# Where a modulation vector is summed: strips of the matmul array, or VectorE beside a feed-forward part; and the order of a product in four strips

## The chip, the cores and the metric

The kernel runs on one core of one Trainium2 chip, in float32 throughout (large products as three float32r products of split operands). The time is device microseconds of that core for one execution of the whole two-layer program; lower is better.

## What is computed

Two layers of a backbone over 512 latent tokens and 256 context tokens, width 1024. Of each layer these lines matter here: the modulation vector `mod` comes from the conditioning alone, and the decays of the gated linear attention (GLA) come from a projection to 32 columns.

```
mod   = (silu(c)     @ w_ada[l] + b_ada[l])          # 1024 -> 6 x 1024, one row
mod_c = (silu(c_ctx) @ w_ada[l] + b_ada[l])          # the context tokens' row
sh_m, sc_m, gt_m, sh_f, sc_f, gt_f = split(mod, 6)
h  = rmsnorm(x, norm_mix[l]) * (1 + sc_m) + sh_m      # hc with mod_c
... = split_projection(h @ w_in[l])                   # g_a: 32 columns, 2 x rank 16
y_a = window_attention(...); y_c = neighbourhood_attention(...)
gf  = log_sigmoid(g_a[:, :16] @ gla_gate_w_fwd + b) / 16   # gb from g_a[:, 16:]
y_b = gla_output(gla_bidirectional(..., gf, gb), g_r)
x = x + gt_m * merge_branches(h, y_a, y_b, y_c, ...)
x = x + gt_f * swiglu(rmsnorm(x, norm_ffn[l]) * (1 + sc_f) + sh_f, w_ffn_in[l], w_ffn_out[l])
```

`w_ada[l]` does not depend on the tokens, so the second layer's `mod` can be computed at any time before that layer's first norm. Units 0 and 1 of six (shift and scale of the first norm) are wanted first; the last, `gt_f`, only in the second layer's feed-forward part.

## The kernel before

Activations lie transposed, 128 channels in partitions and up to 768 tokens along the free axis; a product works through blocks of 128 output columns with `KT` = 8 tiles of the inner dimension. Each weight block is loaded into one of three raw buffers `wr` (line 300), and split into a high part on ScalarE (`wh`, line 323) and a low part on VectorE (`wl`, line 326), two blocks ahead. `gemm` runs three matmuls per inner tile (high x high, high x low, low x high).

The program is a list of items; `run_items` walks it. Small work (norms, GLA, attention) is written as generators that `tick` advances by a clock of the program's own: a matmul adds its columns times 0.417 ns (float32r) or 1 ns (float32), a quarter of it for 32-row strips (line 209). After that a scheduler may still move instructions on each engine's queue, as far as data and buffers allow; each engine then runs its queue in order, SP's loads too. So the order in which the program is built is not the order of the code.

Order of stages: first norm and lead of layer 1; GLA beside the gates' products (`zgates`); attention beside more of these; the merge (`merge_items`), where the three branches are weighted and projected out; the feed-forward part (`ffn_items`); then the second layer. The second layer's lead, `gla_lead`, overlaps the end of the first layer's feed-forward part: the norm of the latent tokens, the inner-rank product `gemm_low` on 512 tokens, key and query products, then the same on 256 tokens.

**The modulation vector.** `ada(l, units)` makes for each unit of 1024 columns eight raw items, one for each inner tile: a load of 128 x 1024 (512 KB) through `wr`, and four matmuls of 256 columns with the silu'd conditioning (`cpad`, 32 columns of which two are filled) as the stationary operand, each in its own 32-column strip of the array. They add up in one PSUM buffer `g` over the eight items. Then ScalarE copies the sum (`ada`), and `ada_cols` turns it into columns with two matmuls by `k_sel`. `weave` spreads the items among weighted ones. For the second layer, units 0 and 1 lie in the first layer's attention and units 2 to 5 in the second layer's GLA; the first layer's own units lie in its start and its GLA.

**The inner-rank product.** `gemm_low` takes the weight block `w_ga` (raw, 32 columns for each inner tile) and for each inner tile multiplies the high and then the low half of the activations, in strip `kt % 4`; the four strips' sums are added later by the decays' product with `gw`, whose rows repeat. High and low of one tile thus stand next to each other in one strip.

In the merge, `split` (lines 1487 to 1490 and 168, 169) prepares the first branch's four tiles: a sigmoid on ScalarE, two multiplies on VectorE, a rounded copy on ScalarE, and the remainder on VectorE; the first products wait for them. In a norm, `rstd_rows` (lines 597 to 601) is a chain of small VectorE steps on the token sums, and `norm` (lines 643 to 655) scales and splits tile by tile.

## Time and profile before

| | us |
|---|---|
| median of 3 runs (2550.47 to 2551.61) | 2550.47 |
| the profiled execution, in all | 2551.31 |
| its span | 2549.5 |
| TensorE busy in it | 2477.0 |
| VectorE busy | 1370.3 |
| ScalarE busy | 1040.4 |

The span runs from the first to the last instruction of the program; 1.8 us lie around it. In the profile PE is TensorE, PEld its weight loads (which run beside the matmuls), DVE VectorE, ACT ScalarE, POOL GpSimd and SP the queue that issues the loads. A float32 matmul leaves two records, so four matmuls are x8 in a timeline. Matmuls overlap in their records: what one costs is read from the distance of the starts, not from its length. In tile names `g` and `h` are PSUM buffers of products, `o` and `s` of small work, `T` activations.

### The profile page before, as it was taken

The numbers are of one execution on the slowest core, as the hardware profiler recorded it, in microseconds if no ns is written. First come the engines' busy times: TensorE is split into PE (matmuls) and PEld (weight loads), VectorE is DVE, ScalarE is ACT, GpSimd is POOL, SyncE is SP. The second block draws the span as 40 slices with busy tenths as digits, with TensorE's granted clock in tenths as the row PEclk, the third lists the DMA queues.
The fourth block names the chain that finished last, engine by engine and source line by source line (L and its number), as shares of the span: only waits on it lengthen the run. The fifth ranks groups of instructions, "written<-read, shape, count | busy, mean of one in ns | idle before, by whom it ended". The sixth has DMA issues, their size and how long they took to land.

```text
span 2549.5 us, 39666 instructions
## 1 busy us (share of the span) xinstructions
PE 2477.0 (97%) x15548; PEld 2082.1 (82%) x15548; DVE 1370.3 (54%) x2814; ACT 1040.4 (41%) x1717; POOL 344.4 (14%) x439
## 2 busy tenths in 40 slices
PE   6999999999999999999999999999999999999998
PEld 3777888888888888888888867677888879988887
DVE  4765457647656673222322367646657668633336
ACT  3643345546564452212212245435545566422223
POOL 0231113203213010000000022212313210000000
PEclk9999999999999999999999999899999999999999
DMA  6433543232346332121121344444333276433223
GB/s 229 137 121 116 179 142 98 93 106 81 89 158 221 124 117 90 58 67 66 59 67 62 98 132 133 153 162 119 102 93 86 82 231 191 156 93 99 92 94 120
DMA packets 116427, 300.53 MB, mean 118 GB/s; under 512 B 21520, under 2 KB 31504, under 8 KB 116240
## 3 DMA queue, kind: packets, MB, share of 16 engines
q1 hardware_dynamic: 116240, 297.99, 36.3%
q8 instruction: 122, 2.00, 0.3%
q14 instruction: 65, 0.53, 0.1%
HBM read 258.61 MB, written 29.57 MB: 113 GB/s over the span
## 4 chain that ended last, share of the span: by engine, by line
PE 83%; DVE 8%; ACT 3%; DMA 3%; issue 1%; SPq 1%; POOL 0%; DVEq 0%; ACTq 0%; POOLq 0%
PE g L211 45%; PE h L211 26%; PE s L211 6%; PE s L215 3%; PE o L211 3%; DVE wl L326 1%; DMA wr<-in_w_merge_dram 1%; ACT wh L323 1%; DMA wr<-in_w_in_dram 1%; DVE qd L915 1%; DVE SS L925 0%; DMA T<-zd 0%; DVE T L645 0%; DVE T L582 0%; DVE P L1288 0%
## 5 line engine op out<-in xcount | busy, mean ns | idle before, releaser
L211 PE MATMUL g<-T,wh 128*128 128x512 f32 (+1 forms) x4684 | 1239.3, 352 | 9.1 <-ACT T L720 4.5
L211 PEld LDWEIGHTS g<-T,wh 128*128 128x128 f32 x4684 | 802.1, 190 | 131.1 <-issue 15.8
L211 PE MATMUL g<-T,wl 128*128 128x512 f32 (+1 forms) x2342 | 814.3, 348 | 2.7 <-DVE wl L326 2.5
L211 PE MATMUL h<-T,wh 128*128 128x512 f32 (+1 forms) x2612 | 659.2, 343 | 5.0 <-ACT T L168 4.8
L323 ACT CAST wh<-wr 128x1024 fp32r<-128x1024 f32 (+2 forms) x355 | 344.4, 971 | 711.5 <-PE h L211 263.9
L326 DVE TENSOR_TENSOR wl<-wr,wh 128x1024 fp32r<-128x1024 f32 (+2 forms) x355 | 406.8, 1146 | 380.5 <-ACT wh L323 364.2
L211 PEld LDWEIGHTS h<-T,wh 128*128 128x128 f32 x2612 | 449.6, 189 | 71.4 <-ACT T L168 6.8
L211 PEld LDWEIGHTS g<-T,wl 128*128 128x128 f32 x2342 | 444.8, 190 | 61.6 <-DVE wl L326 4.4
L211 PE MATMUL h<-T,wl 128*128 128x512 f32 (+1 forms) x1306 | 446.3, 342 | 2.5 <-DVE wl L326 2.5
L211 PEld LDWEIGHTS h<-T,wl 128*128 128x128 f32 x1306 | 246.4, 189 | 33.2 <-DVE wl L326 2.9
L1267 ACT ACTIVATE P<-P,sm 128x513 f32<-128x513 f32 (+3 forms) x160 | 115.9, 725 | 127.7 <-DVE sm L1309 113.3
L1272 POOL TENSOR_SCALAR P<-P,sm 128x512 f32<-128x512 f32 (+1 forms) x160 | 112.3, 703 | 387.4 <-DVE sm L1271 357.7
L1322 DVE TENSOR_TENSOR ptl<-s,pth 128x512 fp32r<-128x512 f32 (+1 forms) x144 | 107.9, 749 | 39.0 <-ACT pth L1321 37.8
L652 POOL TENSOR_TENSOR T<-T,T 128x256 f32<-128x256 f32 (+1 forms) x24 | 30.0, 1272 | 731.2 <-DVE T L1552 532.0
L1321 ACT CAST pth<-s 128x512 fp32r<-128x512 f32 (+1 forms) x144 | 90.6, 629 | 46.9 <-PE s L215 43.5
L1552 DVE SCALAR_TENSOR_TENSOR T<-h,mod,T 128x512 f32<-128x512 f32 (+1 forms) x64 | 38.4, 599 | 109.9 <-PE h L211 109.3
L215 PE MATMUL s<-k_ident,P 128*128 128x128 f32 x640 | 94.0, 273 | 1.7 <-POOL P L1272 1.2
L173 ACT CAST T<-T 128x512 fp32r<-128x512 f32 (+1 forms) x93 | 49.1, 536 | 106.7 <-DVE T L1571 100.0
L918 POOL TENSOR_TENSOR E<-E,T 128x512 f32<-128x512 f32 (+1 forms) x42 | 58.4, 1401 | 239.6 <-ACT E L914 212.0
L215 PEld LDWEIGHTS s<-k_ident,P 128*128 128x128 f32 x640 | 74.7, 140 | 16.3 <-issue 4.7
L211 PE MATMUL o<-pth,V 128*128 128x512 f32 (+2 forms) x224 | 72.4, 332 | 0.2 <-ACT pth L1321 0.2
L211 PE MATMUL o<-ptl,V 128*128 128x512 f32 (+2 forms) x224 | 70.8, 332 | 1.1 <-DVE ptl L1322 1.1
(200 smaller groups left out, 2253.7 us busy)
## 6 DMA issues: line engine op xcount, KB each, us to landing
wr<-in_w_fi_dram SPq DMA_DIRECT2D x98, 512.0 KB, 3.5
wr<-in_w_ada_dram SPq DMA_DIRECT2D x80, 512.0 KB, 4.2
wr<-in_w_in_dram SPq DMA_DIRECT2D x65, 512.0 KB, 3.8
wr<-in_w_merge_dram SPq DMA_DIRECT2D x48, 512.0 KB, 4.2
wr<-in_w_out_dram SPq DMA_DIRECT2D x32, 512.0 KB, 3.6
wr<-in_w_fo_dram SPq DMA_DIRECT2D x32, 512.0 KB, 3.5
wr<-in_w_br_dram SPq DMA_DIRECT2D x48, 256.0 KB, 3.0
wr<-in_w_fo_dram SPq DMA_DIRECT2D x32, 384.0 KB, 3.0
```

Source lines behind the costliest of these rows:

```text
L173: self.nc.scalar.copy(hi, src)
L211: return self.nc.tensor.matmul(out, lhsT, rhs, **kw)
L215: return self.nc.tensor.transpose(out, src, self.ident)
L323: self.nc.scalar.copy(hi[:, :n], r[:, :n])
L326: self.nc.vector.tensor_tensor(out=lo[:, :n], in0=r[:, :n], in1=hi[:, :n].bitcast(F32), op=ALU.subtract)
L652: nc.gpsimd.tensor_tensor(out=t[:, w], in0=x[kt][:, w], in1=r[:, w], op=ALU.mult)
L918: P.tensor_tensor(out=ee[:, 1, c0:c1], in0=ee[:, 1, c0:c1], in1=self.gk[p][:, t0:t0 + c1 - c0], op=ALU.mult)
L1267: nc.scalar.activation(out=P_[:, o0:e1], in_=P_[:, o0:e1], func=AF.Exp, bias=nm_, accum_out=rz)
L1272: nc.gpsimd.tensor_scalar(out=P_[:, o0:o1], in0=P_[:, o0:o1], scalar1=rz, scalar2=1.0, op0=ALU.mult, op1=ALU.mult)
L1321: nc.scalar.copy(hi, src)
L1322: return lambda: VE.tensor_tensor(out=lo, in0=src, in1=hi.bitcast(F32), op=ALU.subtract)
L1552: self.nc.vector.scalar_tensor_tensor(out=x[:, c0:c1], in0=ps[:, :c1 - c0], scalar=self.mod[l][:, sec * 8 + j, s:s + 1], in1=x[:, c0:c1], ...
```

## The change

`ada` is no longer called for the second layer. In its place a generator `ada_late` is started in the first layer's feed-forward part, after the first two weight pairs. For each unit, half of its columns (512) and inner tile it loads 128 x 512 (256 KB) into one of two buffers `wad`, and VectorE multiplies it by the tile's conditioning value, a scalar per partition, once for the latent and once for the context row: a multiply for the first inner tile, a multiply-add into `wac` for the other seven. After eight tiles the 128 partitions are added on TensorE: for each of the two rows four matmuls of 128 columns in the four strips, by `sel`, which has one column of ones. ScalarE copies the result, and after both halves `ada_cols` turns it into columns as before. Between the steps the generator asks for 4.5 of the program's clock.

In `gemm_low` the eight inner tiles go in two halves of four; in each, the four high halves go to the four strips in turn, then the four low halves. The number of matmuls is the same.

```diff
--- before.py
+++ after.py
@@ -423,6 +423,11 @@
         self.cpad = self.cp.tile([128, KT, 32], F32, name="cpad")
         nc.gpsimd.memset(self.cpad, 0.0)
         nc.scalar.activation(out=self.cpad[:, :, 0:2], in_=cs, func=AF.Silu)
+
+        self.sel = self.cp.tile([128, 2, 32], F32, name="sel")
+        nc.gpsimd.memset(self.sel, 0.0)
+        for s in range(2):
+            nc.gpsimd.memset(self.sel[:, s, s:s + 1], 1.0)
         self.mod = [self.cp.tile([128, 48, 2], F32, name=f"mod{l}") for l in range(DEPTH)]
         self.gain = [self.cp.tile([128, 2, 8, 2], F32, name=f"gain{l}") for l in range(DEPTH)]
         self.nmix, self.nffn, self.bada, self.bmerge, self.gbias, self.gnorm, self.sink = ([] for _ in range(7))
@@ -485,6 +490,47 @@
                     self.tick()
                 self.items.append(Item(fn, self.a["w_ada"][l, n, kt], 8, raw=True))
 
+    def ada_late(self, l):
+
+
+        nc = self.nc
+        sb = None
+        todo = [(n, h, kt) for n in range(6) for h in range(2) for kt in range(KT)]
+
+        def load(q):
+            n, h, kt = todo[q]
+            t = self.ph.tile([128, 512], F32, tag="wad", name=self.nm("wad"), bufs=2)
+            nc.sync.dma_start(t, self.a["w_ada"][l, n, kt][:, 512 * h:512 * h + 512])
+            return t
+        w = load(0)
+        for q, (n, h, kt) in enumerate(todo):
+            nxt = load(q + 1) if q + 1 < len(todo) else None
+            if kt == 0:
+                acc = self.ph.tile([128, 2, 512], F32, tag="wac", name=self.nm("wac"), bufs=1)
+            for s in range(2):
+                c = self.cpad[:, kt, s:s + 1]
+                if kt == 0:
+                    nc.vector.tensor_scalar(out=acc[:, s], in0=w, scalar1=c, scalar2=None, op0=ALU.mult)
+                else:
+                    nc.vector.scalar_tensor_tensor(out=acc[:, s], in0=w, scalar=c, in1=acc[:, s], op0=ALU.mult,
+                                                   op1=ALU.add)
+            w = nxt
+            yield 4.5
+            if kt < KT - 1:
+                continue
+            ps = self.gemm_psum()
+            for s in range(2):
+                for g in range(4):
+                    self.matmul(ps[32 * g:32 * g + 32, :128], self.sel[:, s], acc[:, s, 128 * g:128 * g + 128],
+                                start=s == 0, stop=s == 1, tile_position=(0, 32 * g))
+            if h == 0:
+                sb = self.base.tile([128, 256], F32, tag="ada", name=self.nm("ada"), bufs=1)
+            nc.scalar.copy(sb[:, 128 * h:128 * h + 128], ps[:, :128])
+            yield 1.5
+            if h == 1:
+                self.ada_cols(l, n, sb, True)
+                yield 0.5
+
     def adp_tile(self):
         if not self.begun:
             return self.pp.tile([128, 512], F32, tag="a", name=self.nm("a"), bufs=1)
@@ -496,13 +542,14 @@
             return self.pp.tile([128, 512], F32, tag="h", name=self.nm("h"))
         return self.ps.tile([128, 512], F32, tag="g", name=self.nm("g"), bufs=3)
 
-    def ada_cols(self, l, n, sb):
+    def ada_cols(self, l, n, sb, late=False):
+
         nc = self.nc
         pm = self.O1()
 
         for j in range(2):
-            self.matmul(pm[:, :16].rearrange("p (g j s) -> p j g s", j=2, s=2)[:, j], sb[:, j * 128:j * 128 + 128],
-                        self.c["k_sel"], start=True, stop=True)
+            o = pm[:, 8 * j:8 * j + 8] if late else pm[:, :16].rearrange("p (g j s) -> p j g s", j=2, s=2)[:, j]
+            self.matmul(o, sb[:, j * 128:j * 128 + 128], self.c["k_sel"], start=True, stop=True)
 
         def gain(sec, b0, b1):
             j = (SC_M, SC_F).index(sec)
@@ -751,12 +798,14 @@
             mov = self.hmov(l, 0, c)
             n = c[1] - c[0]
             ps = self.gemm_psum()
-            for kt in range(KT):
-                xh, xl = mov(kt)
-                r, s = slice(32 * (kt % 4), 32 * (kt % 4) + 32), slice(32 * kt, 32 * kt + 32)
-                for x, first, last in ((xh, kt < 4, False), (xl, False, kt >= 4)):
-                    self.matmul(ps[r, :n], w[:, s], x.bitcast(F32), start=first, stop=last,
-                                tile_position=(0, 32 * (kt % 4)))
+
+            for half in range(2):
+                hl = [mov(kt) for kt in range(4 * half, 4 * half + 4)]
+                for x in range(2):
+                    for g in range(4):
+                        r, s = slice(32 * g, 32 * g + 32), slice(128 * half + 32 * g, 128 * half + 32 * g + 32)
+                        self.matmul(ps[r, :n], w[:, s], hl[g][x].bitcast(F32), start=half == 0 and x == 0,
+                                    stop=half == 1 and x == 1, tile_position=(0, 32 * g))
             self.ahead()
             if c[0] == 0:
                 tile_()
@@ -1586,6 +1635,8 @@
             for c in sets:
                 for t in range(lead):
                     pair(t, [c])
+            if lead and l < DEPTH - 1:
+                self.do(lambda: self.add(self.ada_late(l + 1)))
             for t in range(t0 + lead, t0 + tn):
                 pair(t, subs_of)
             w = lambda j: self.a["w_fo"][l, j][:, t0 * 128:(t0 + tn) * 128]
@@ -1690,7 +1741,7 @@
             self.do(begin)
             if l == 0:
                 self.do(self.consts_rest)
-            side = self.cap(lambda: self.ada(l, range(2, 6)))
+            side = self.cap(lambda: self.ada(l, range(2, 6))) if not last else []
             main = self.cap(lambda: (self.gla_items(l), self.zgates(l, range(0, ZS[l][0]), ntok)))
             self.weave(main, side)
 
@@ -1702,11 +1753,10 @@
                 self.ztag = "z"
                 self.attn_open(l)
             self.do(to_attn)
-            side = self.cap(lambda: self.ada(1, (0, 1))) if not last else []
             main = self.cap(lambda: (self.attn_a_items(l), self.gate_r(l), self.zgates(l, range(*ZS[l]), ntok),
                                      self.attn_c_items(l, ntok),
                                      self.zgates(l, range(ZS[l][1], 24), ntok)))
-            self.weave(main, side)
+            self.items += main
             self.do(self.close_phase)
             self.do(self.ada_flush)
             self.merge_items(l, (lambda: a["xT"]) if l == 0 else (lambda: self.xs[0]), ntok)
```

How the built program's order changes is shown at three places. On VectorE at the start of the first layer's merge, where the four tiles of the first branch are split (multiplies by `gnorm` and by the result, and the remainder with shape 128x768), the order before is:

```order
L169 TENSOR_TENSOR T_7817<-T_7796,T_7816 128x768
L1488 SCALAR_TENSOR_TENSOR T_7804<-T_7804,gnorm_728,T_7820 128x768
L1490 TENSOR_TENSOR T_7797<-T_7797,T_7804 128x768
L169 TENSOR_TENSOR T_7825<-T_7797,T_7824 128x768
L1488 SCALAR_TENSOR_TENSOR T_7807<-T_7807,gnorm_728,T_7828 128x768
L1490 TENSOR_TENSOR T_7798<-T_7798,T_7807 128x768
L169 TENSOR_TENSOR T_7833<-T_7798,T_7832 128x768
L1488 SCALAR_TENSOR_TENSOR T_7810<-T_7810,gnorm_728,T_7836 128x768
L1490 TENSOR_TENSOR T_7799<-T_7799,T_7810 128x768
L169 TENSOR_TENSOR T_7841<-T_7799,T_7840 128x768
```
and now:

```order
L169 TENSOR_TENSOR T_7707<-T_7686,T_7706 128x768
L1537 SCALAR_TENSOR_TENSOR T_7694<-T_7694,gnorm_732,T_7710 128x768
L1539 TENSOR_TENSOR T_7687<-T_7687,T_7694 128x768
L169 TENSOR_TENSOR T_7715<-T_7687,T_7714 128x768
L513 TENSOR_SCALAR wac_9736<-wad_9732,cpad 128x512 x2
L1537 SCALAR_TENSOR_TENSOR T_7697<-T_7697,gnorm_732,T_7718 128x768
L515 SCALAR_TENSOR_TENSOR wac_9736<-wad_9734,cpad,wac_9736 128x512
L1539 TENSOR_TENSOR T_7688<-T_7688,T_7697 128x768
L515 SCALAR_TENSOR_TENSOR wac_9736<-wad_9734,cpad,wac_9736 128x512
L515 SCALAR_TENSOR_TENSOR wac_9736<-wad_9776,cpad,wac_9736 128x512
L169 TENSOR_TENSOR T_7723<-T_7688,T_7722 128x768
L1537 SCALAR_TENSOR_TENSOR T_7700<-T_7700,gnorm_732,T_7726 128x768
```
Eight of the new steps stand between the second and the fourth tile's remainder (five in these rows, three behind them); each pair needs its load.

On VectorE in the second layer's lead, from the last squares of the context tokens (`T`, 128x256) through the small chain of the root (`nsm`), the order before is:

```order
L582 TENSOR_TENSOR T_13253<-T_13253,T_13745 128x256
L326 TENSOR_TENSOR wl_13759<-wr_13699,wh_13758 128x1024
L1552 SCALAR_TENSOR_TENSOR T_8515<-g_13748,mod_75,T_8515 128x256
L582 TENSOR_TENSOR T_13253<-T_13253,T_13774 128x256
L597 TENSOR_SCALAR nsm_13819<-o_13816 128x2
L185 TENSOR_SCALAR nsm_13819<-nsm_13819 128x2
L188 TENSOR_TENSOR nsm_13819<-nsm_13819 128x2
L189 SCALAR_TENSOR_TENSOR nsm_13819<-nsm_13819 128x2
L190 SCALAR_TENSOR_TENSOR nsm_13819<-nsm_13819 128x2
```
and now (line numbers of the changed file):

```order
L629 TENSOR_TENSOR T_13610<-T_13610,T_14141 128x256
L513 TENSOR_SCALAR wac_14162<-wad_13990,cpad 128x512 x2
L326 TENSOR_TENSOR wl_14155<-wr_14084,wh_14154 128x1024
L1601 SCALAR_TENSOR_TENSOR T_8405<-h_14144,mod_79,T_8405 128x256
L515 SCALAR_TENSOR_TENSOR wac_14162<-wad_14160,cpad,wac_14162 128x512
L629 TENSOR_TENSOR T_13610<-T_13610,T_14175 128x256
L515 SCALAR_TENSOR_TENSOR wac_14162<-wad_14160,cpad,wac_14162 128x512
L644 TENSOR_SCALAR nsm_14224<-o_14221 128x2
L515 SCALAR_TENSOR_TENSOR wac_14162<-wad_14217,cpad,wac_14162 128x512
L185 TENSOR_SCALAR nsm_14224<-nsm_14224 128x2
L326 TENSOR_TENSOR wl_14243<-wr_14172,wh_14242 128x1024
L188 TENSOR_TENSOR nsm_14224<-nsm_14224 128x2
```
The steps on `wac` of the last half unit stand ahead of that chain and inside it, and two weights' low parts have come with them.

On TensorE in the second layer's lead, at the first inner-rank product (strips of 32 rows, 512 columns), high and low half of a tile alternate before:

```order
L211 MATMUL h_13785<-T_13609,wr_13603 32x512
L211 MATMUL h_13785<-T_13610,wr_13603 32x512
L211 MATMUL h_13785<-T_13621,wr_13603 32x512
L211 MATMUL h_13785<-T_13622,wr_13603 32x512
L211 MATMUL h_13785<-T_13637,wr_13603 32x512
L211 MATMUL h_13785<-T_13638,wr_13603 32x512
L211 MATMUL h_13785<-T_13656,wr_13603 32x512
L211 MATMUL h_13785<-T_13657,wr_13603 32x512
```
and now four tiles' high halves stand ahead of their low halves:

```order
L211 MATMUL g_14186<-T_13994,wr_13984 32x512
L211 MATMUL g_14186<-T_14006,wr_13984 32x512
L211 MATMUL g_14186<-T_14022,wr_13984 32x512
L211 MATMUL g_14186<-T_14041,wr_13984 32x512
L211 MATMUL g_14186<-T_13995,wr_13984 32x512
L211 MATMUL g_14186<-T_14007,wr_13984 32x512
L211 MATMUL g_14186<-T_14023,wr_13984 32x512
L211 MATMUL g_14186<-T_14042,wr_13984 32x512
```
So two neighbours no longer share a strip.

## Rows read from the trace of the kernel before

**Rows 1.** The page, part 1: engine, busy us, share of the span, instructions.
```profile
PE 2477.0 (97%) x15548; PEld 2082.1 (82%) x15548; DVE 1370.3 (54%) x2814; ACT 1040.4 (41%) x1717; POOL 344.4 (14%) x439
```

**Rows 2.** Busy time by stretches: stretch, its length, engines, clock, DMA share, GB/s.
```profile
775.00:1445.00 670.00, 666.92 (x3823) 584.53 (x3822) 266.69 (x389) 189.06 (x278) 30.69 (x24) 1.00 0.28 91
...
1516.00:1707.00 191.00, 180.90 (x1496) 132.76 (x1495) 110.41 (x207) 78.78 (x107) 36.37 (x28) 0.92 0.46 153
```

**Rows 3.** TensorE's timeline: start, length, engine, line, tiles, shapes; `ada` items of layer 2.
```profile
412.91 0.64 PE L211 MATMUL g<-wr,cpad 128*32 128x256 f32 x8
413.48 0.73 PE L211 MATMUL g<-T,wh 128*128 128x512 f32 x2
...
1552.52 0.40 PE L211 MATMUL g<-T,wh 128*128 128x256 f32 x2
1552.76 0.28 PE L211 MATMUL g<-T,wl 128*128 128x256 f32 x1
1552.97 1.07 PE L211 MATMUL g<-wr,cpad 128*32 128x256 f32 x16
1553.97 0.50 PE L211 MATMUL g<-T,wh 128*128 128x512 f32 x1
```

**Rows 4.** TensorE's timeline at the start of the first layer's merge.
```profile
750.40 0.64 PE L211 MATMUL g<-wr,cpad 128*32 128x256 f32 x8
751.59 0.58 PE L211 MATMUL o<-k_sel,ada 128*128 128x8 f32 x4 [0.55 <-ACT ada L483]
753.35 0.50 PE L211 MATMUL h<-T,wh 128*128 128x512 f32 x1 [1.18 <-ACT T L168]
```

**Rows 5.** TensorE's timeline: four float32 matmuls of 128 columns, and the next.
```profile
1473.86 1.13 PE L211 MATMUL o<-dg,ones 128*128 128x128 f32 x8 [0.23 <-DVE dg L601]
1474.75 0.36 PE L211 MATMUL h<-T,wl 128*128 128x256 f32 x1
```

**Rows 6.** VectorE's timeline: a multiply and a multiply-add of 128x512.
```profile
73.42 0.42 DVE L885 TENSOR_SCALAR qd<-T 128x512 f32<-128x512 f32 x1
...
1482.55 0.74 DVE L645 SCALAR_TENSOR_TENSOR T<-T,gain,T 128x512 f32<-128x512 f32 x1
```

**Rows 7.** The first merge's start: VectorE, SP's queue; DMA issues by size, us to landing.
```profile
757.11 0.96 DVE L169 TENSOR_TENSOR T<-T,T 128x768 fp32r<-128x768 f32 x1 [0.90 <-ACT T L168]
...
761.95 0.96 DVE L169 TENSOR_TENSOR T<-T,T 128x768 fp32r<-128x768 f32 x1 [1.95 <-ACT T L168]
...
755.52 2.42 SPq L1457 DMA_DIRECT2D T<-zd  x5
...
wr<-in_w_br_dram SPq DMA_DIRECT2D x48, 256.0 KB, 3.0
...
T<-zd SPq DMA_DIRECT2D x24, 384.0 KB, 4.8
```

**Rows 8.** The second layer's lead: VectorE ahead of the second norm.
```profile
1496.08 0.42 DVE L582 TENSOR_TENSOR T<-T,T 128x256 f32<-128x256 f32 x1 [1.57 <-ACT T L581]
1498.43 0.16 DVE L597 TENSOR_SCALAR nsm<-o 128x2 f32<-128x2 f32 x1 [1.93 <-PE o L211]
```

**Rows 9.** Waits of TensorE from 1516 to 1707 us: total, times, longest.
```profile
PE g L211 <- ACT wh L323: 4.3, 4, 2.3
...
PE s L211 <- DVE T L896: 1.8, 1, 1.8
PE g L211 <- DVE wl L326: 1.5, 2, 1.2
```

**Rows 10.** The inner-rank product in the second layer: TensorE, then VectorE.
```profile
1484.71 4.65 PE L211 MATMUL h<-T,wr 128*32 128x512 f32 x22
1490.30 0.62 PE L211 MATMUL h<-T,wr 128*32 128x512 f32 x2 [0.94 <-DVE T L655]
...
1491.96 0.68 DVE L655 TENSOR_TENSOR T<-T,T 128x512 fp32r<-128x512 f32 x1
```

**Rows 11.** A stretch at the lower clock in the second layer's GLA (columns as in rows 2).
```profile
1647.00:1667.00 20.00, 20.00 (x89) 15.28 (x89) 5.60 (x11) 3.22 (x4) 1.33 (x1) 0.50 0.10 31
```

## The prediction

> **What bounds the kernel now.** I read the busy times of the engines first: TensorE is busy 2477.0 of 2549.5 us and VectorE 1370.3 [rows 1]. So a microsecond of TensorE work is worth a microsecond wherever TensorE does not wait, and VectorE has room on average. The average hides stages, so next the table by stretches [rows 2]: from 775 to 1445 us (the end of the first layer's merge and its feed-forward part) TensorE is busy 666.92 of 670 us and VectorE 266.69; from 1516 to 1707 (the second layer's gated linear attention, GLA) TensorE is busy 180.90 of 191 at a mean granted clock of 0.92. Third come the single matmuls of the modulation vector, fourth the places where TensorE waits. The diff takes TensorE work out of the first layer's attention and the second layer's GLA, and puts VectorE work and a little TensorE work into the feed-forward part, which has 403 us of idle VectorE.
>
> **What is removed.** One item of `ada` is four strip matmuls of 256 columns, eight records in the trace. A pair of items starts 0.21 us after the matmul ahead of it, where two such matmuls take 0.24 (1552.52 to 1552.76), and the next weights' matmul starts 1.00 later: 1.09 for two, 0.55 each [rows 3]. One item alone holds TensorE 0.57, and with the same 0.09 ahead 0.66. The second layer's six units are 48 items. 16 (units 0 and 1) lie one by one in the first layer's attention; the last, at 750.40, stands ahead of TensorE's waits of 0.55 and 1.18 us [rows 4] and is hidden, so 15 x 0.66 = 9.9. The other 32 lie in the second layer's GLA, by the program's order 26 in pairs and 6 alone: 26 x 0.55 + 6 x 0.66 = 18.3. Four of the six column turns (`k_sel`, 0.58 us each at 751.59 [rows 4], 0.6 with its start) go out of these stages too, one from attention and three from GLA: 2.4. Together 30.6 us, in stages where TensorE waits little.
>
> **What is added on TensorE.** Twelve sums over partitions, each eight strip matmuls of 128 columns with `sel`, and the six column turns, all in or next to the feed-forward part, where TensorE never stands. The trace has no such sum. A float32 matmul of 128 columns over the whole array takes 0.22 (eight records, 1473.86 to 1474.75 [rows 5]), so eight take 0.44 if four strips run side by side and 1.78 one after another, plus the start. As columns they are what one item was, so I take the lone item's 0.66, the row nearest to them: 12 x 0.66 = 7.9 (bounds 6 to 23). With 6 x 0.6 = 3.6 for the turns 11.5 us. Net of this and the removal: **-19.1 us**.
>
> **What is added on VectorE.** 96 half tiles, each multiplied by two scalars: for one unit's half 2 multiplies and 14 multiply-adds, the first 0.42 and the second 0.74 us by the rows of the same shapes [rows 6]: 11.2 us, 134 in all. In the feed-forward part that is hidden: VectorE has 403 us to spare, the weights' low parts are made two weights ahead, and one weight there is 48 matmuls at 670 / 3823 us each [rows 2], 8.4 us, far more than two steps of 0.74. If the cover were gone, every step would cost its 0.74. ScalarE's twelve small copies in place of six lie in the same stretch (189 of 670 us busy), and three memsets on GpSimd (14% busy [rows 1]) come at the program's start. But the order is not that of the code: the scheduler has moved the first unit's half up to the merge's start and the last one down into the second layer's lead.
>
> The **merge's start** (first layer) is a place where TensorE waits for VectorE and ScalarE: it waits 1.18 for the first tile's split [rows 4], and VectorE idles 1.95 ahead of the third [rows 7]. In the changed order VectorE has eight of the new steps between the second and the fourth tile's low part, and the loads of the second to fifth tile stand on SP's queue, with two buffers, each behind VectorE's release. The gates' loads go out at 755.52 and take 4.8 us at the median for 384 KB; 256 KB take 3.0 [rows 7]. So the first tile lands at about 759.5 where VectorE is ready at 758 (after the second tile's low part, 757.11), then two multiplies (0.8), two to four multiply-adds (0.7 net of overlap) minus the idle time that is there: the fourth split is about 3.5 us late, and so are the gate loads queued behind. Bounds: 1.3 (the two steps ahead of the third tile alone) and 8 (two of the loads waited for in full). **+3.5**.
>
> In the **second layer's lead** sixteen steps stand on VectorE from the end of the first norm on, some inside the small chain that makes the second norm's root, for which VectorE idles 1.57 and 1.93 in the run before [rows 8]. Eight of them (2 x 0.42 + 6 x 0.7 = 5.0) come before the second norm's scaling, three more inside it (2.1); less those 3.5 of idle time and with about 1 us for the sum at the end: **+4.5** (1 to 8). This half unit is wanted only in the second layer's feed-forward part; its cost is its place alone.
>
> **What goes with the removal.** In GLA TensorE waits 4.3 for a weight's high part and 1.5 for its low part [rows 9]: the items share the three raw buffers with the weights. Without them most of that goes: **-4** (0 to -5.8). What is late next is GLA's own chain: its steps are spaced by the program's clock, in which an item counted 0.26 us though it took 0.55 to 0.66, so each step loses some 0.3 to 0.4 us of cover. One such wait of 1.8 is there already [rows 9]: **+3** (0 to 15, if the chain ended every step).
>
> **The inner-rank product.** Before, 11 strip matmuls of 512 columns take 4.65 us (22 records), 0.42 each: two side by side at most, since high and low half of a block follow each other in one strip [rows 10]. Then TensorE waits 0.94 for the norm, whose last low half comes at 1492.64. With four strips in turn TensorE only arrives earlier at that wait; what it does meanwhile is the next weight's matmuls, which are there in both orders. I count 0.5 us for each of the second layer's two calls and 0.5 for the first layer's second: **-1.5** (0 to -10). [...]
>
> **Sum.** -19.1 + 3.5 + 4.5 - 4 + 3 - 1.5 = -13.6. The profiled execution took 2551.3 us in all (span 2549.5); 2551.3 - 13.6 = 2537.7, **2538 us**. The median is 2550.5, 0.8 below the profiled execution, too little to shift it. Less than 0.2% (5 us) either way I call no change.
>
> **Rivals.**
> [...]
> (b) *A wait in place of the one removed* (0.18): GLA's chain keeps half to all of the 18.3, 9 to 18, so 6 to 15 come back beyond the 3 counted: 2544 to 2553. For it: 110 of 191 us on VectorE and the 1.8 wait; against: 1.8 is the only one of its kind there.
> (c) *The clock, slower* (0.11): in this GLA the granted clock stands at 0.50 from 1647 to 1667 us [rows 11], and the mean of 0.92 over 191 us makes it 30 us in all, after strip and 64-wide products and a wait of 1.8 us. If the steps without cover wait like that at each scan and product, half the time in such a stretch is lost: with 40 us more at 0.50 the cost is 20, and 2538 + 20 = 2558. It decides from 36 us more on. [...]
> (d) *The strips do not overlap* (0.06): the new sums run one after another, 12 x (1.96 - 0.66) = 15.6 more: 2554, no change.
>
> **How the numbers follow.** Forecast 0.50, all of it faster; (a) 0.15 faster; (b) 0.07 faster, 0.11 same; (c) 0.11 slower; (d) 0.05 same, 0.01 slower. Faster 0.72, same 0.16, slower 0.12. The range runs from somewhat under (a), 2524, well into (b), 2551: left out are (c), (d) and the outer part of (b), 0.2 together.
>
> **What would show it.** In the changed trace: no `cpad` matmul in the first layer's attention or the second layer's GLA; twelve groups of `sel` strips of about 0.66 us each (serial ones: near 2); a busy VectorE from 775 to 1445 near 390 us with TensorE still full; a longer wait than 1.18 to 1.4 at the merge's start; a wait for VectorE at the second norm of the lead; in GLA fewer waits on high and low weight parts and a stage some 19 us shorter, at a granted clock not below 0.92. I am wrong if the feed-forward part grows by much more than 11 us (VectorE or SP held weights up), if GLA shrinks by under 10, or if its clock falls.

## The result, and the profile after

The changed kernel takes **2517.56 us** (median of 4 runs, 2517.06 to 2520.49), the kernel before beside it 2550.54 (2550.47 to 2551.61): ratio 0.987, 95% interval 0.9853 to 0.9888. It is 33 us faster, where I had forecast 13.6 and a range that ended at 2524. The profiled execution of the changed kernel took 2517.52 us, its span is 2515.7; that is 33.8 less than the profiled execution of before, and the ledger below is made of these two.

Part 1 of the page of the changed kernel answers [rows 1]; the line of part 5 is the new multiply-add (count, busy time, mean ns, idle time ahead and what ended it):

```profile
PE 2441.8 (97%) x15356; PEld 2068.8 (82%) x15356; DVE 1484.7 (59%) x3006; ACT 1043.1 (41%) x1723; POOL 345.9 (14%) x442
...
L515 DVE SCALAR_TENSOR_TENSOR wac<-wad,cpad,wac 128x512 f32<-128x512 f32 x168 | 119.1, 747 | 24.1 <-DMA wad<-in_w_ada_dram 23.8
```

TensorE is 35.2 us less busy, VectorE 114.4 us more. Next the stretches that answer [rows 2] in the changed kernel: the feed-forward part, the second layer's GLA, and three short stretches inside that GLA (stretch, length, busy time of PE, PEld, DVE, ACT, POOL, clock, DMA share, GB/s):

```profile
927.00:1472.00 545.00, 544.77 (x3249) 475.64 (x3248) 273.81 (x410) 128.20 (x196) 3.45 (x4) 1.00 0.35 111
...
1529.00:1717.00 188.00, 178.02 (x1380) 142.36 (x1378) 122.57 (x226) 84.83 (x114) 39.20 (x33) 0.97 0.28 87
...
1546.77:1550.18 3.41, 3.41 (x9) 2.64 (x8) 1.65 (x6) 3.25 (x5) 0.06 (x1) 0.50 0.06 23
1560.42:1563.83 3.41, 3.41 (x12) 2.83 (x11) 3.41 (x9) 0.00 (x0) 0.00 (x0) 0.50 0.00 0
1574.07:1577.48 3.41, 3.41 (x13) 2.89 (x12) 1.07 (x2) 2.28 (x3) 1.88 (x3) 0.50 0.07 22
```

The feed-forward part stays full (544.77 of 545). GLA has become 188 us long, and its granted clock is 0.97 instead of the 0.92 of [rows 2]: all that stands at half rate there now (0.50: a 512-column product starts every 0.43 us, as from 1547.24 to 1547.67, and at full rate every 0.23) are these three stretches, 10.2 us; before, it was 30.7.

Where the 33.8 us come from, stage by stage. The marks are the first matmul of a kind in each stage (the first with `gw`, the first with a `Q`, the first of the merge, the norms' `dg`, 910.2 and 1473.9 before); "at half" is the time at 0.50 in the stage. Two products change stage by the built order, and the table is set right for that: 21 of the gates' 512-column matmuls, 0.23 us each, stand ahead of GLA's mark now and behind it before (4.8 us, left out of both columns), and 24 of 256 columns have crossed the mark between the first layer's GLA and its attention, which are therefore one line. Most of one pair of items (1.0 us, at 1524.6) stands just ahead of GLA's mark before, so its removal is in the lead's line.

| stage | before (at half) | after (at half) | difference |
|---|---|---|---|
| start, up to the first layer's GLA | 82.6 (6.8) | 79.8 (6.8) | -2.7 |
| first layer's GLA, attention, up to the merge's first product | 670.8 (10.2) | 658.3 (3.8) | -12.5 |
| merge, up to the feed-forward part's first norm | 156.9 (0) | 159.7 (6.5) | +2.8 |
| feed-forward part | 563.6 (0) | 573.9 (0) | +10.3 |
| second layer's lead | 51.7 (0) | 52.2 (0) | +0.4 |
| second layer's GLA | 220.2 (30.7) | 188.4 (10.2) | **-31.8** |
| from there to the end | 799.0 | 798.6 | -0.4 |

### The profile page after: what moved, and what is told of

Same layout as the page of the kernel before. It is cut to its first block, busy times and chain, and to the rows that moved or that the text cites. A ratio compares the mean times of both kernels' runs of the same rounds, so it can differ in the third digit from the quotient of the medians.

```text
span 2515.7 us, 39662 instructions
## 1 busy us (share of the span) xinstructions
PE 2441.8 (97%) x15356; PEld 2068.8 (82%) x15356; DVE 1484.7 (59%) x3006; ACT 1043.1 (41%) x1723; POOL 345.9 (14%) x442
## 5 line engine op out<-in xcount | busy, mean ns | idle before, releaser
L211 PEld LDWEIGHTS g<-T,wh 128*128 128x128 f32 x4672 | 801.9, 190 | 118.4 <-issue 13.6
L515 DVE SCALAR_TENSOR_TENSOR wac<-wad,cpad,wac 128x512 f32<-128x512 f32 x168 | 119.1, 747 | 24.1 <-DMA wad<-in_w_ada_dram 23.8
L1601 DVE SCALAR_TENSOR_TENSOR T<-h,mod,T 128x256 f32<-128x256 f32 (+1 forms) x67 | 40.0, 597 | 85.6 <-PE h L211 85.5
```

The costliest lines, as they stand in the source:

```text
L211: return self.nc.tensor.matmul(out, lhsT, rhs, **kw)
L515: nc.vector.scalar_tensor_tensor(out=acc[:, s], in0=w, scalar=c, in1=acc[:, s], op0=ALU.mult, op1=ALU.add)
L1601: self.nc.vector.scalar_tensor_tensor(out=x[:, c0:c1], in0=ps[:, :c1 - c0], scalar=self.mod[l][:, sec * 8 + j, s:s + 1], in1=x[:, c0:c1], ...
```

## The experiments

My theory before them: the forecast's terms hold, and the missing 20 us lie in the second layer's GLA, where the granted clock no longer falls for so long. Rivals: the new order of the inner-rank product did it; attention gained more than its items cost; the strip matmuls themselves bring the clock down; the loads through the weights' buffers do.

### One part at a time

Units 0 and 1 alone summed late:

```diff
...
-                self.do(lambda: self.add(self.ada_late(l + 1)))
+                self.do(lambda: self.add(self.ada_late(l + 1, (0, 1))))
...
-            side = self.cap(lambda: self.ada(l, range(2, 6))) if not last else []
+            side = self.cap(lambda: self.ada(l, range(2, 6)))
```


> Units 0 and 1 alone are summed late (the strips' new order is in); units 2 to 5 stay as items in the second layer's GLA. Theory (the unforecast part sits in the second layer's GLA, because its items are gone, as granted clock and weight waits): attention -13, the start of layer 1 -4.6, merge +5, four sums and two turns in the feed-forward part +3.5, the GLA of layer 2 as in the kernel before with its 30 us at half rate: about 2541 us (2537 to 2545). Rival (the new order of the inner-rank product changes what follows, and so the GLA's clock, whatever the items do): GLA shorter by 10 here already, 2531. Rival (attention gained more than the 9.9 + 0.6 that the items cost): attention 13 or more shorter here, as in the full change; if it depends on GLA it is not.

Units 2 to 5 alone:

```diff
...
+                self.do(lambda: self.add(self.ada_late(l + 1, range(2, 6))))
...
-            self.items += main
+            self.weave(main, self.cap(lambda: self.ada(1, (0, 1))) if not last else [])
```


> Units 2 to 5 alone are summed late; units 0 and 1 stay as items in the first layer's attention. Theory: the second layer's GLA is 36 us shorter, as in the full change (its stretches at half rate 10 us instead of 30), feed-forward part +7, merge start and lead as in the full change +5 and +5, attention unchanged, start -4.6: about 2527 us (2523 to 2531). Rival (the shorter GLA comes from something ahead of it, in attention or the lead, not from its own items): GLA only 18 to 20 us shorter, 2543.

Only the inner-rank product's new order in the kernel before, and all but that order in the changed kernel (the same edit, one way and the other):

```diff
-            for kt in range(KT):
-                for x, first, last in ((xh, kt < 4, False), (xl, False, kt >= 4)):
...
+            for half in range(2):
...
+                for x in range(2):
+                    for g in range(4):
...
```


> The kernel before with only the new order of the inner-rank product. Theory: -1.5 to -6, all of it in the first layer's start and GLA and in the two calls of the second layer's lead: 2544 to 2549 us; the second layer's GLA unchanged with 30 us at half rate. Rival (the order brings the GLA its clock): 2535 or less. [...]

> The changed kernel with the old order of the inner-rank product (high and low half of a tile in the same strip). Theory: it is worth 1.5 in the second layer's lead and the 2.7 to 4.6 by which the first layer's start and GLA are earlier: 2520 to 2524 us, GLA of the second layer as short as in the changed kernel, at a granted clock of 0.97. Rival (the new order brings the GLA its clock): half rate back to some 30 us there, 2532 or more. Rival (the strips overlapped before already): 2517.5 to 2518.5.

Raw marks are those of each kernel, with the 21 products where they stand; on them GLA is 225.0 long in the kernel before and 188.4 in the changed one.

| | median us | ratio to before, 95% | GLA, raw marks (at half) |
|---|---|---|---|
| units 0, 1 late | 2540.19 | 0.9937 to 0.9967 | 214.8 (10.2) |
| units 2 to 5 late | 2520.30 | 0.9854 to 0.9913 | 189.1 (6.8) |
| new product alone | 2545.54 | 0.9959 to 0.9991 | 214.8 (13.7) |
| all but the new product | 2522.58 | 0.9864 to 0.9920 | 189.4 (10.2) |

The medians of the first, third and fourth lie where the theory put them. The second came out 3 us below its range: the lead, which I had down for +5, gave 1.0 there, since 64 steps end ahead of it. GLA falls to 189 whenever its own items are gone, with the old product too, and to no such value otherwise: the product's order and attention are out as causes. In the first layer the stages up to the merge are 11.2 us shorter with units 0 and 1 gone and 2.0 without that, of which 1.7 are half rate.

In two of these profiles the items are in GLA and the half rate is short (10.2 and 13.7). They are the second fastest of 10 runs (2533.6) and the fastest of 10 (2537.8), 7 us below their medians, so they show that the long half rate can stay away, not that it usually does. That needed repeats.

### Is the half rate chance?

> The kernel before unchanged, for a second profile of its second GLA. Theory (the half rate there is there in most executions, since its waits are the same in each): 25 us or more at half rate in GLA and 2549 to 2556 us. Rival (the 30.7 us of the first profile were chance): 10 to 15 us at half rate in GLA at a time of 2540 to 2545.

> As e_before_2, a third profile of the kernel before. The two together with the first tell how far time and half rate go together: by the theory that the time differs between executions through the granted clock alone, the time less half of all half rate is the same within 1.5 us in all three (2551.3 less half of 58.3: 2522.2).

> The changed kernel unchanged, a second profile. Theory: half rate in its second GLA near 10 us again (3 to 14), time 2517 to 2521; if it reaches 25 us or more, the difference of the clock between the two kernels was chance.

The kernel before took 2556.08 and 2552.20 us in these, the changed one 2517.53. GLA stood at half rate for 30.7 us in both profiles of before, in the same three pieces (6.8, 3.4, 20.5) as in the first, and for 10.2 in that of the changed kernel, again three of 3.4. So the difference belongs to the kernels. The other executions on record say how firmly: of 48 of the kernel before, 44 ran at a granted clock of 0.985 to 0.990 over the whole program (2545.3 to 2559.5 us) and four at 0.991 to 0.994 (2540.6 to 2545.0); all five of the changed kernel stood at 0.991 to 0.994. Units 0 and 1 late and the new product alone, which keep the items in GLA, stood at 0.990 or less in 8 of 10 each. The long half rate is thus usual in the kernel before, not certain; no profile is of one of its four fastest executions.

Time less half of all half rate is 2522.2, 2523.0 and 2520.9 in the three of before (2.1 apart, somewhat more than I allowed) and 2498.0 in both of the changed kernel: 24 us of the 34 are there at full clock. Over the 48 executions, whose times lie 19 us apart, the time less the clock's share (one less the granted clock, times the span) lies between 2518.0 and 2525.4. (The ledger at the end gives the clock more than the other 10, since the changed kernel's new 6.8 us at half rate at the merge's start cost nothing there, as a run below shows.)

The stretches of the second profile of before, GLA and its three pieces (columns as above):

```profile
1529.00:1755.00 226.00, 213.52 (x1661) 159.82 (x1659) 128.16 (x233) 88.72 (x120) 39.33 (x33) 0.93 0.46 149
1544.60:1551.40 6.80, 5.40 (x13) 4.35 (x14) 4.93 (x9) 4.81 (x6) 1.79 (x1) 0.50 0.26 80
1626.50:1629.90 3.40, 3.40 (x9) 2.63 (x9) 2.79 (x7) 0.00 (x0) 0.90 (x1) 0.50 0.75 202
1650.40:1670.80 20.40, 20.40 (x90) 15.20 (x89) 4.72 (x8) 3.22 (x4) 1.32 (x1) 0.50 0.14 49
```

And TensorE's timeline at the long piece in that profile (start, length, engine, line, tiles, shapes, wait ahead of it and what ended it):

```profile
1647.38 0.40 PE L211 MATMUL g<-T,wl 128*128 128x512 f32 x1
1649.59 0.46 PE L211 MATMUL s<-T,PP 64*128 64x128 f32 x2 [1.81 <-DVE T L896]
1649.97 0.87 PE L211 MATMUL g<-T,wh 128*128 128x512 f32 x2
...
1651.63 0.79 PE L211 MATMUL s<-gst,SS 64*128 64x128 f32 x2
...
1653.07 0.79 PE L211 MATMUL s<-gst,PP 64*128 64x128 f32 x2
1653.66 0.63 PE L211 MATMUL s<-gst,SS 64*128 64x128 f32 x2
1654.22 0.79 PE L211 MATMUL s<-gv,A 128*128 128x128 f32 x2
...
1666.19 1.13 PE L211 MATMUL s<-qd,E 64*64 64x64 f32 x32
1667.25 0.79 PE L211 MATMUL g<-T,wh 128*128 128x512 f32 x1
...
1671.33 0.40 PE L211 MATMUL g<-T,wl 128*128 128x512 f32 x1
```

TensorE waits 1.81 us for VectorE right ahead of GLA's state products (`PP`, `SS`, `gst`, 64 and 128 rows by 128 columns). At 1650.4, while four of the gates' products run behind the first `PP`, the clock falls to 0.50. The row of small products from 1651.63 to 1667.25 runs at half rate, and the clock rises at 1670.9, when the gates' 512-column products have been running again since 1667.25. This wait is the one of 1.8 in [rows 9], this stretch that of [rows 11].

In the changed kernel the same state products have no wait ahead of them. Its wait of that kind (1.37) stands 47 us earlier, among the gates' products:

```profile
1590.29 0.62 PE L211 MATMUL g<-T,wh 128*128 128x512 f32 x2
1592.29 0.84 PE L211 MATMUL s<-gv,E 128*64 128x128 f32 x10 [1.37 <-DVE T L945]
...
1638.98 0.48 PE L211 MATMUL s<-T,PP 64*128 64x128 f32 x2
1639.30 0.38 PE L211 MATMUL s<-gst,SS 64*128 64x128 f32 x2
1639.62 0.49 PE L211 MATMUL s<-gv,A 128*128 128x128 f32 x2
1640.04 0.48 PE L211 MATMUL s<-gst,PP 64*128 64x128 f32 x2
```

From a `PP` product to the `SS` product behind it it takes 0.32 here and 0.59 above: the same products at the two clocks. The changed kernel still waits in this GLA (total, times, longest), longer at a time than in [rows 9], and for its own chain alone:

```profile
PE s L215 <- POOL SS L1004: 3.0, 2, 2.3
PE s L215 <- DVE gv L854: 2.6, 1, 2.6
PE s L215 <- ACT T L767: 2.3, 1, 2.3
PE s L211 <- DVE T L945: 1.4, 1, 1.4
```

A fall to 0.50 follows each of the first three, but each time the gates' products come next, and it lasts 3.4 us.

Such a wait is not always followed by a fall. In the kernel with the shorter step (below) TensorE waits 2.56 us ahead of the same `SS` product, and the granted clock is 1.00 from 1560 to 1600:

```profile
1571.02 0.44 PE L215 MATMUL s<-k_ident,SS 128*128 128x128 f32 x2 [2.56 <-POOL SS L1004]
...
1560.00:1600.00 40.00, 34.74 (x317) 27.71 (x316) 32.85 (x63) 14.43 (x22) 16.77 (x11) 1.00 0.20 60
```

Nor did one follow waits of 2.27 us (all but the new product), 2.35 (own buffers, below) and 2.09 (step and tie, below). The length of a wait alone does not decide.

### Matmuls or loads?

The items' two halves, put back into the changed kernel's GLA one at a time: the strips without loads, the loads without strips, and whole items with buffers of their own.

```diff
...
+    self.matmul(self.adp[r, :256], self.cpad[:, kt, :], self.cpad.rearrange("p k s -> p (k s)"), ...
...
```


> The changed kernel, and in the second layer's GLA 32 items as before put back as matmuls alone: four strips of 256 columns each on a tile that is already there, no loads, and every eighth followed by the copy to ada; their sums are not used. Cost of the matmuls themselves 32 x 0.55 to 0.66 = 18 to 21 us. Theory A (the strips on a mostly empty array lower the granted clock): half rate back to about 30 us, 10 us more: 2546 to 2549. Theory B (the loads in the weights' buffers were what cost the clock and the waits): the matmuls alone, 2536 to 2538, half rate stays near 10 us. Theory C (items fill waits of GLA's chain): under 2534.

```diff
...
+    self.matmul(self.adp[:, :2], w[0][:, :128], self.cpad[:, kt, :2], ...      # w: the item's load
...
```


> The changed kernel, and in the second layer's GLA the 32 loads of 512 KB through the weights' three buffers put back, each released by one full-array matmul of two columns in the item's place (about 0.15 to 0.3 us each, 5 to 10 us in all) instead of the strips; their sums are not used. Theory A (the strips lower the clock): 2523 to 2528, half rate near 10 us, some weight waits (up to 5.8 us) back. Theory B (the loads cause the waits and these the fall of the clock): weight waits of 4 to 6 us and half rate near 30 us: 2537 to 2544.

```diff
...
+    t = self.ph.tile([128, 1024], F32, tag="wi", name=self.nm("wi"), bufs=2)
+    self.nc.sync.dma_start(t, self.a["w_ada"][l, n, kt])
...
```


> The changed kernel, and in the second layer's GLA the 32 items of units 2 to 5 put back whole (load of 512 KB, four strip matmuls, copy), but with two load buffers of their own instead of the weights' three; their columns are not used. Theory (the items cost their matmuls, 17 to 19 us; what they did beyond that, weight waits of 6 us and the long half rate that followed one of them, came through the weights' buffers): no waits on weight parts in GLA, half rate 7 to 14 us there, 2535 to 2538 us in little spread. Rival (items with loads bring the half rate whatever buffers they use): 25 us or more at half rate, 2543 to 2548.

Then only the eight items around the long stretch: their loads taken out of the kernel before (their matmuls read a tile that is already there), and the eight alone put into the changed one.

```diff
+                dry = l == 1 and n == 4
...
-                self.items.append(Item(fn, self.a["w_ada"][l, n, kt], 8, raw=True))
+                self.items.append(Item(fn) if dry else Item(fn, self.a["w_ada"][l, n, kt], 8, raw=True))
```


> The kernel before, but the eight items of the second layer's unit 4 (which stand around the long stretch at half rate) multiply a tile that is already there instead of loading theirs: same matmuls in the same places, no loads through the weights' buffers for these eight; unit 4's columns are not the right ones. Theory (the wait for a weight's high part behind these loads, 1.8 to 2.3 us, brings the 20.5 us at half rate): the wait and the stretch are gone, half rate in GLA 10 to 14 us, and the time some 12 us shorter, 2538 to 2543 us. Rival (the stretch comes with the strips or by the place in GLA): half rate stays at 25 to 31 us, 2549 to 2553.

```diff
-            side = self.cap(lambda: self.ada(l, range(2, 6))) if not last else []
+            side = self.cap(lambda: self.ada(l, range(2, 6))) if not last else (
+                [Item(lambda: None)] * 16 + self.cap(lambda: self.ada(l, (4,))) + [Item(lambda: None)] * 8)
```


> The mirror of it: the changed kernel with only the eight items of unit 4 put back into the second layer's GLA, whole and through the weights' buffers, at the same point of the weave. Eight items cost 8 x 0.55 = 4.4 us and a turn 0.6. Theory (the weight wait behind such loads brings the long half rate): a weight wait of some 2 us and half rate of 25 us or more in GLA: 2531 to 2535 us. Rival (it takes all 32 items, or another state of GLA): half rate near 10 us as in the changed kernel, 2522 to 2526.

GLA in these profiles, all on the changed kernel's marks (a 512-column matmul that stands on the other side counted at 0.23); "at full" is its length less half of the time at half rate; the last column is the wait straight ahead of the state products. Of the 32 items two stand ahead of the mark in the kernels with strips or loads alone, most of one pair in the kernel before, with or without unit 4's loads, and none with own buffers:

| kernel | median us | GLA | at half | at full | waits for weights | wait ahead of the state |
|---|---|---|---|---|---|---|
| before | 2550.5 | 220.2 | 30.7 | 204.9 | 5.8 | 1.81 |
| before, unit 4 without loads | 2537.9 | 204.5 | 6.8 | 201.1 | 2.6 | 1.21 |
| after, 32 items in own buffers | 2545.1 | 207.6 | 6.8 | 204.2 | 0 | 1.16 |
| after, 32 strips, no loads | 2535.1 | 203.9 | 6.8 | 200.5 | 0 | 1.16 |
| after, 32 loads, no strips | 2537.4 | 205.3 | 17.1 | 196.8 | 6.8 | none |
| after, unit 4's items | 2527.8 | 198.1 | 10.2 | 193.0 | 3.4 | none |
| after | 2517.6 | 188.4 | 10.2 | 183.3 | 0 | none |

The strips' row falls out at once: 200.5 - 183.3 = 17.2 us at full clock for the 30 items behind the mark, 0.57 each, and no long half rate; all five executions of that kernel stood at a granted clock of 0.992 to 0.994. A pair in that kernel starts 0.32 after the matmul ahead and the next one follows 1.00 later, as in [rows 3]:

```profile
1601.21 0.39 PE L211 MATMUL g<-T,wl 128*128 128x512 f32 x1
1601.53 1.07 PE L211 MATMUL g<-cpad 128*32 128x256 f32 x16
1602.53 1.98 PE L211 MATMUL s<-T,gw 128*128 128x512 f32 x4
```

So in this GLA the strips without loads do not bring the long half rate (6.8 us at half); the theory that they do is out. Unit 4 says what the loads did in the kernel before: without eight of them the same 32 items' matmuls run in the same places, the waits for weights fall from 5.8 to 2.6, the wait ahead of the state products from 1.81 to 1.21, and the 20.5 us at half rate are gone, with the piece of 3.4. GLA is 15.7 us shorter, 12 of them by the clock. All four executions of that kernel stood at a granted clock of 0.992 or 0.993, six of the seven of the kernel before beside them at 0.987 or 0.988. So in the kernel before the loads of these eight items bring the long half rate. In the profile of the run without them:

```profile
1641.68 0.39 PE L211 MATMUL g<-T,wl 128*128 128x512 f32 x1
1643.28 0.46 PE L211 MATMUL s<-T,PP 64*128 64x128 f32 x2 [1.21 <-DVE T L900]
...
1645.62 0.48 PE L211 MATMUL s<-gst,PP 64*128 64x128 f32 x2
1645.95 0.38 PE L211 MATMUL s<-gst,SS 64*128 64x128 f32 x2
```

The mirror did not come true. Unit 4's items in the changed kernel bring their weight waits back (0.89 and 0.53 at the first pair, below), and cost 9.7 us where their matmuls and the turn are 5; but no wait stands ahead of the state products, and the half rate stays at 10.2.

```profile
1620.99 1.07 PE L211 MATMUL g<-wr,cpad 128*32 128x256 f32 x16
1622.95 0.73 PE L211 MATMUL g<-T,wh 128*128 128x512 f32 x2 [0.89 <-ACT wh L323]
1624.21 0.50 PE L211 MATMUL g<-T,wl 128*128 128x512 f32 x1 [0.53 <-DVE wl L326]
```

My expectation that the wait for a weight starts the long half rate did not hold: the weight waits came back and the long half rate did not. What the profiles fit is that it starts behind the wait for VectorE at the state products, and that the loads set how long that is in the kernel before. This is argued from the places and not shown, since no run took that wait alone away. It was 1.81 in the three profiles with the fall; in the other five that have it, it was 0.81 (new product alone), 1.16 twice, 1.21 and 1.68 (units 0, 1 late), without a fall. Own buffers show that the weight waits are not the whole price either: with none of them GLA is still 204.2 at full clock, since other waits come in (3.5 for the gate's weights, 3.2 in the chain):

```profile
PE s L211 <- DMA gw<-in_gate_w_dram: 3.5, 1, 3.5
PE s L215 <- ACT T L797: 3.2, 2, 2.3
```

That kernel's time missed my expectation by 7 us for reasons outside GLA: its start stood 17.1 us at half rate in this profile and was 3.7 longer than the changed kernel's, and its lead was 3.4 longer. The loads without strips brought the weight waits back in full (6.8 us) and a time in the range of theory B, but half rate only half-way, 17.1 us in four pieces, and that in the execution with the lowest granted clock of its five (0.989; the others 0.990 to 0.994).

### Two places that give back

Only a shorter step:

```diff
-            yield 4.5
+            yield 4.0
```


> The changed kernel with 4.0 instead of 4.5 of the program's clock for each step: the last half unit ends ahead of the second layer's lead, the first one still stands in the merge's start. Theory: the lead's +5 is gone and nothing else moves: 2511 to 2514 us. Rival (the lead is late for another reason): 2517 to 2519.

The shorter step, and the first step tied to the feed-forward part:

```diff
...
+        cv = self.cp.tile([128, KT, 2], F32, name="cv")
+        nc.vector.scalar_tensor_tensor(out=cv, in0=src[:, 0:16].rearrange("p (k s) -> p k s", s=2), scalar=0.0,
+                                       in1=self.cpad[:, :, 0:2], op0=ALU.mult, op1=ALU.add)
...
-                c = self.cpad[:, kt, s:s + 1]
+                c = cv[:, kt, s:s + 1]
...
-            yield 4.5
+            yield 4.0
...
-                self.do(lambda: self.add(self.ada_late(l + 1)))
+                self.do(lambda: self.add(self.ada_late(l + 1, st["u"][0][0].bitcast(F32))))
```


> The changed kernel with the late sums held out of two places: the scalars are taken from a copy that depends on the first feed-forward tile, so that no step can stand in the first layer's merge, and a step asks for 4.0 of the program's clock instead of 4.5, so that the last one stands ahead of the second layer's first norm. Theory (merge start, merge and lead pay for the steps on VectorE; the half rate of 6.8 us at the merge's start follows the wait there): merge start -2.4, merge -2.9 , half rate there gone, lead -5: 2507 to 2511 us. Rival (what is given back there comes from elsewhere: the order of the lead, or the clock falls at another place): 2515 to 2520.

The first gave 2514.73 us (ratio 0.9829 to 0.9881), a little above its range; the second **2509.96** (0.9812 to 0.9865), 7.6 below the changed kernel and the fastest of all. Held out of the merge, the steps no longer cost their 2.7 there (157.0, before 156.9); with the shorter step the lead is 3.5 shorter (set right for the products on its mark) and the feed-forward part 1.6 longer. One expectation failed: the half rate at the merge's start stays (6.8 us, 4.5 of them behind the merge's first product, where they cost nothing that can be seen: 157.0 against 156.9). The timeline there, in that kernel, with no new step in the merge:

```profile
735.93 0.51 PE L211 MATMUL o<-k_sel,ada 128*128 128x8 f32 x4
...
740.67 0.80 PE L211 MATMUL h<-T,wh 128*128 128x512 f32 x1 [4.23 <-ACT T L168]
```

and in the changed kernel:

```profile
733.44 0.51 PE L211 MATMUL o<-k_sel,ada 128*128 128x8 f32 x4
738.16 0.79 PE L211 MATMUL h<-T,wh 128*128 128x512 f32 x1 [4.22 <-ACT T L168]
```

The wait has the same length with and without the steps on VectorE, so they do not make it. ScalarE's order and TensorE's last product ahead of the merge, in the kernel before and in the changed one:

```profile
747.80 1.28 ACT L1487 ACT_TABLE_LOAD   x1
749.10 0.85 ACT L1487 ACTIVATE T<-T 128x768 f32<-128x768 f32 x1
750.19 0.28 PE L211 MATMUL g<-T,wl 128*128 128x256 f32 x1
...
732.59 1.28 ACT L1536 ACT_TABLE_LOAD   x1
733.88 0.84 ACT L1536 ACTIVATE T<-T 128x768 f32<-128x768 f32 x1
733.32 0.28 PE L211 MATMUL g<-T,wl 128*128 128x256 f32 x1
```

From the sigmoid to the merge's first product it takes 4.3 us in both (to 753.35 and 738.16). But its table load stood 2.4 us ahead of TensorE's last product before and stands 0.7 ahead now, and the last item with its turn, which filled part of the wait, is gone. So the way from that product to the merge is 4.8 us instead of 3.2.

## Why the prediction was wrong, step by step

| term | forecast | measured | from |
|---|---|---|---|
| attention's items and one turn | -10.5 | -9.1 | line 2 of the stage table less 3.4 of clock; the 1.7 by which the merge's first product is later behind attention is in it |
| steps in the merge | +3.5 | +2.8 | stage table; 0.1 without them |
| sums and turns, feed-forward part | +11.5 | +10.3 | stage table |
| steps in the lead | +4.5 | +3.8 | +0.4 less the product's -2.4 and the pair's -1.0 |
| items, turns, weight waits, chain in GLA | -21.1 | -22.5 | 204.9 to 183.3 at full clock, and 1.0 for the pair ahead of the mark |
| inner-rank product | -1.5 | -5.1 | -2.7 in the start, -2.4 in the lead |
| granted clock | 0 | **-13.7** | GLA 30.7 to 10.2 at half: -10.3; first layer's GLA and attention 10.2 to 3.4: -3.4 |
| the end | 0 | -0.4 | |
| sum | -13.6 | -33.9 | |

**The step that failed is the clock.** The sum counted it at nothing, and let it in only as rival (c), in the slower direction, "if the steps without cover wait like that at each scan and product". I had the stretch at half rate [rows 11], the 30 us it makes with its neighbours, and the wait of 1.8 [rows 9] on the table, and treated half rate as a property of the stage, which could only become more. In all three profiles of before 20.5 of the 30.7 us stand behind one wait, and most of that (15.6 us, 1651.63 to 1667.25) is a row of small products that runs at half rate throughout. The change took away the loads that bring this stretch (unit 4 without loads: 30.7 to 6.8), and the changed kernel has no wait there. The granted clock was 0.97 where I had said "not below 0.92": the text named the sign of being wrong downwards only. Of the 20.2 us missed, 13.7 are this.

**The price that rival (c) used was right**: half the time of such a stretch. From a `PP` product to the `SS` behind it it takes 0.59 us there and 0.32 at full rate, and the 48 executions above lie 19 us apart, less the clock's share 7.4. Its direction was not: I had let waits without cover bring more half rate. The rows do not bear that out: TensorE's busy share in GLA is 178.02 of 188, 94.7%, against 213.52 of 226, 94.5%, practically the same, at 10.2 and 30.7 us of half rate, and in the long stretch TensorE was busy for 20.40 of 20.40 us and stood at 0.50.

**The inner-rank product** was undervalued: -5.1 instead of -1.5. I had argued that TensorE only comes earlier to a wait. The first ten strips now take 3.6 us, eleven took 4.65 [rows 10], so the free strips give little in the call of 512 columns; TensorE then waits 1.41 instead of 0.94:

```profile
1482.65 3.60 PE L211 MATMUL g<-T,wr 128*32 128x512 f32 x20
1487.66 1.05 PE L211 MATMUL g<-T,wr 128*32 128x512 f32 x2 [1.41 <-ACT T L694]
```

That far the argument held for the second layer. The gain there lies in the call of 256 columns: with the new product alone in the kernel before, it begins 0.2 us earlier and ends 2.8 earlier. In the first layer that call begins 1.6 earlier and ends 2.5 earlier, so 1.6 come from the call of 512 columns ahead of it, which I had put at nothing, and 0.9 from it. No run shows a call that halves, on which this term's bound of -10 and (a) of the chances rested: ten strips of 512 columns take 0.36 us each now and took 0.42 before, and the new order is worth 5.1 in all. One over the whole array would take about 0.88 (an estimate, four times the 0.22 of [rows 5]); by that some two ran side by side before, and some two and a half now.

**What held.** The removal and the GLA's own terms came out to 1.4 us at full clock; that is partly luck in its parts. The items' matmuls are 17.2 for 30 of them, at 0.57 each 18.3 for 32, as forecast. The weight waits went entirely, 5.8 instead of 4. The chain waited more, as I had said: 9.7 us in all (with 0.4 on `E`) against 5.4 by the same view of before, +4.3 where I had counted +3. Rival (b), the chain taking back 9 to 18, is refuted. The sums are what I took for them: 0.57 from start to start for eight strips of 128 columns, so rival (d) is out:

```profile
1092.77 0.64 PE L211 MATMUL g<-wac,sel 128*32 128x128 f32 x16
1093.34 0.50 PE L211 MATMUL g<-T,wh 128*128 128x256 f32 x2
```

VectorE's steps are hidden as forecast: 0.75 us for a multiply-add, 23.8 us of waiting for their loads in all, with TensorE full beside them. VectorE is busy 361 of 671 us in the like stretch, 762 to 1433, where I had said near 390. The merge's **reason** was half wrong: the longer wait at its start is there with or without the steps (4.23 and 4.22; ScalarE starts the split later against attention's end, and the item that I had called hidden and so free no longer fills the gap), and the steps cost their 2.8 later in the merge.

**What stays open.** Why the wait ahead of the state products is 1.81 us in the kernel before and 1.21 without eight loads, in terms of VectorE's queue; and what besides the length of a wait decides over a fall: 1.68 there, and 2.09 to 2.56 elsewhere, were followed by none. The first layer's -3.4 of clock was seen (10.2, 13.7 and 10.2 us at half rate up to the merge's first product in the three profiles of before, 3.8 in both of the changed kernel) but not tried by itself. Whether removing that one wait alone, with all loads kept, frees the 20.5 us wasn't tried.

## What to carry to other kernels

Work that fills a stage with waits is worth its own matmuls, and beside that whatever its loads do to the others' buffers: here eight items cost 9.7 us where their matmuls and turn cost 5. Where the granted clock of a stage is under 1, list its stretches at half rate before forecasting, look at what TensorE did ahead of each and what it runs in it, and give the clock a term with both signs: in this kernel a wait of 1.8 us ahead of a row of small products was followed by 20.5 us at half rate, waits of 2.1 to 2.6 ahead of the gates' products by 3.4 to 6.8 or by none. Where a scheduler may hoist work into another stage, tie it to a value of the stage that it was meant for (here 7.6 us together with a shorter step, which alone gave 2.8).

## What the hardware showed that I had not expected

- The same row of small products ran at half rate from 1651.6 to 1667.3 with TensorE busy throughout (20.40 of 20.40 us of the stretch), and at full rate throughout in the changed kernel and without unit 4's loads (0.32 and 0.33 us from a `PP` product to the `SS` behind it, against 0.59); the rate came back at 1670.9, among the 512-column products that follow.
- Waits of 2.3 to 2.6 us in the changed kernel's GLA were followed by 3.4 us at half rate each, so by about 1.7 us of loss beside the wait itself; waits of 2.1 to 2.6 in four other kernels by none.
- The half rate repeats from execution to execution, though not always: three stretches of 6.8, 3.4 and 20.5 us in GLA in each of three profiles of the kernel before, three of 3.4 in both of the changed kernel; and 44 of 48 executions of the kernel before at a granted clock of 0.990 or less, four above.
- Ten strips of 512 columns that go round the four strips take 3.6 us, 0.36 each, against 0.42 where neighbours share a strip.
